# Sums of two weight blocks on VectorE: each tied behind the corrections that precede it in the program

## The chip, the cores and the metric

One core of one Trainium2 chip. The kernel is a single launch; its time is device microseconds of that core, lower is better. A TensorE clock is granted by the throttle and shown by the profile as a share of full speed.

## The reference

A decoder trunk of two layers on 256 tokens of width 2048, in float32: a layer with gated linear attention, a layer with sliding-window attention and sinks, each followed by an MLP of width 8192. What matters here are the large products, all with weights that are read from HBM once:

```python
def sqrelu_mlp(h, w1, w2):
    u = jax.nn.relu(h @ w1)
    return (u * u) @ w2

for layer in range(DEPTH):
    u = rmsnorm(h, norm_mix[layer])
    h = h + mixer(u, ...)                       # GLA in layer 0, windowed attention in layer 1
    h = h + sqrelu_mlp(rmsnorm(h, norm_mlp[layer]), mlp_w1[layer], mlp_w2[layer])
```

## The kernel before

**Weights in two parts.** TensorE multiplies in a reduced float32 format, so each weight block of 512x512 (a tile of 128x2048 in SBUF) is split: ScalarE casts it to a rounded copy `wh`, VectorE subtracts that from the block and leaves the correction `wl`. `halve` does this in two halves of 128x1024 each: two casts (line 116) and two corrections (line 117). Activations are split in the same way. A product of a block with one tile of 128 tokens is then 12 matmuls of 512 columns: for each of four slices k one with `wh`, one with `wl`, one more with `wh` and the activations' small part. The second matmul of each three is the first that needs the correction.

**Rings.** `wh` has 4 tiles of half a block (two blocks), so a block's casts can start only when TensorE is done with the block two before it, half by half. `wl` and the weight tiles `ws` have 3 buffers each.

**Seven products.** Pairs of block columns use Strassen's scheme in Winograd's form: a 2x2 arrangement of blocks b11, b12, b21, b22 needs seven products instead of eight, with sums of weight blocks as operands. A sum is formed in place by VectorE (128x2048, or two halves of 128x1024), and some sums by a DMA that accumulates into the tile `wx`. Besides the seven-product part there are "plain" blocks, which multiply all 256 tokens (24 matmuls). The scheme is written twice:

- `Seven` for the columns of the gated layer's v and r (heads 2 and 3), of two residual projections, and of the MLP's first matrix (`two_columns`, 14 times). The order of its steps is a string, such as `1 21 3 7 5 31 x 20 e 6 2 30 a 4`: a single digit is a product, two digits a plain block, x and the steps 7 and 2 form sums.
- `seven`, for the MLP's second matrix, 16 times: for each of two layers, four groups g of rows, two pairs n of columns. Its order on TensorE is: product 0, plain (2,1), product 2, plain (3,1), products 4 and 6, plain (2,0), plain (3,0), then product 5, product 1 (with b21) and product 3 (with the last sum). The prediction calls the last three products 5, 2 and 4, as `Seven` does; and it calls the b12 product (`product("C", 6, b12)`) by the name of its block.

**Three kinds of sums.** b12 += b22 (lines 307 and 1193), x += b22 (lines 322 and 1198; in the heads and the residual projections a DMA does it) and x += b21 (lines 331 and 1211). The last needs x's product 5 or 6 to have been split first, and b21 to have been loaded; b21 itself is the operand of product 2, and the sum x that of product 4.

**What sets the order.** The program is written in the order of the work; a scheduler puts it into one queue for each engine. `tc.high_priority(offset=WPRI)`, with WPRI = 60, lets an instruction stand ahead of its place by 60 steps of priority; loads, casts, corrections and sums have it, the additions that empty PSUM (lines 1149 and 1150) mostly have not. Each engine runs its own queue in order.

Of the kernel before, what the change touches and what calls it, by code (L numbers as in the profile page):

```python
# [8 lines left out]
F32 = mybir.dt.float32  # L9
# [26 lines left out]
WPRI = 60  # L36
# [15 lines left out]
def yoco_kernel(ctx: ExitStack, tc: tile.TileContext, x, norms, mlp_w1, mlp_w2, a_w_in, w_glr, w_gate, a_g_o, a_w_o,  # L52
                kv_w_k, kv_w_v, kv_g_k, b_w_q, b_g_q, b_sinks, b_w_o, out):
    nc = tc.nc
# [22 lines left out]
    def tick():  # L77
        now[0] += 1
        for fn in due.pop(now[0], ()):
            fn()  # L80

    def mm(o, l, r, start=True, stop=True, **kw):
        nc.tensor.matmul(o, lhsT=l, rhs=r, start=start, stop=stop, **kw)  # L83
# [20 lines left out]
    nc.gpsimd.memset(mhalf, -0.5)  # L104


    def halve(ws, o=C, n=2):

        whs = [wp.tile([P, 2, C], F32R, name="wh", tag="wh", bufs=WHL) for _ in range(2)]
        wl = wp.tile([P, 4, C], F32R, name="wl", tag="wl", bufs=WS)  # L110
        with tc.high_priority(offset=WPRI):
            for k in range(0, 4, n):
                wh = whs[k // 2]
                js, ks = slice(k % 2, k % 2 + n), slice(k, k + n)
                w = ws[k // 2] if isinstance(ws, list) else ws[:, ks, :o]
                nc.scalar.copy(out=wh[:, js, :o], in_=w)  # L116
                nc.vector.tensor_sub(out=wl[:, ks, :o], in0=w, in1=wh.bitcast(F32)[:, js, :o])  # L117
        return [(whs[k // 2][:, k % 2], wl[:, k]) for k in range(4)]

    def split_w(parts, step=4):  # L120
        ws = wp.tile([P, 4, C], F32, name="ws", tag="ws", bufs=WS)
        with tc.high_priority(offset=WPRI):
            for k in range(0, 4, step):
                ks = slice(k, k + step)
                o = 0
                for ap in parts:
                    n = ap.shape[1]
                    nc.sync.dma_start(out=ws[:, ks, o:o + n],
                                      in_=ap[k * P:(k + step) * P].rearrange("(k p) n -> p k n", p=P))
                    o += n  # L130
        return halve(ws, o, min(step, 2))
# [85 lines left out]
    class Seven:  # L217
# [39 lines left out]
        def product(self, b, o, ws):  # L257
            p, st = self.use(b)
            halves = halve(ws)
            for k in range(4):  # L260
                wh, wl = halves[k]
                mm(p, o[0][:, k], wh, st and k == 0, False, skip_group_check=True)
                mm(p, o[0][:, k], wl, False, False, skip_group_check=True)
                mm(p, o[1][:, k], wh, False, k == 3, skip_group_check=True)
            tick()
            return p

        def plain(self, i, j, b0, b1):
            halves = halve(self.load(i, j))
            ps_ = [self.use(b) for b in (b0, b1)]  # L270
            for k in range(4):
                wh, wl = halves[k]
                for t in range(NT):
                    p, st = ps_[t]
                    a, l = self.token(i, t)
                    mm(p, a[:, k], wh, st and k == 0, False, skip_group_check=True)
                    mm(p, a[:, k], wl, False, False, skip_group_check=True)
                    mm(p, l[:, k], wh, False, k == 3, skip_group_check=True)
                if k % 2:
                    tick()  # L280
# [22 lines left out]

        def p7(self, after):
            b12 = self.load(0, 1)
            with tc.high_priority(offset=WPRI):
                nc.vector.tensor_add(out=b12, in0=b12, in1=self.y)  # L307
            after["p7"](self.product("C", self.op(3), b12))

        def ef(self, after):  # L310
# [6 lines left out]
            after["p5"](p)  # L317

        def px(self, after):
            with tc.high_priority(offset=WPRI):  # L320
                for n in range(2):
                    nc.vector.tensor_add(out=self.wx[n], in0=self.wx[n], in1=self.y[:, 2 * n:2 * n + 2])

        def p6(self, after):
            after["p56"](self.product("D", self.op(1), self.wx))

        def p2(self, after):
            b21 = self.load(1, 0)
            with tc.high_priority(offset=WPRI):
                for n in range(2):  # L330
                    nc.vector.tensor_add(out=self.wx[n], in0=self.wx[n], in1=b21[:, 2 * n:2 * n + 2])
            self.product("A", self.token(1, 0), b21)
            if not self.late:
                after["a"](self.banks["A"])

# [616 lines left out]
    def mlp(w1, w2, act, r, gains):  # L952
# [32 lines left out]
        def two_columns(col, es, hs, put, order):  # L985
# [45 lines left out]
            def p4(p):  # L1031
# [5 lines left out]
                      [x[:, 2 * i:2 * i + 2] for i in range(2)],  # L1037
                      lambda: mp.tile([P, 4, C], F32, name="wy", tag="wy", bufs=1))
            z.run({"p1": p1, "p7": p7, "ef": lambda e, f: ef.extend((e, f)), "p5": p5, "p56": p56, "a": p2, "c": p4},
                  order)  # L1040

# [52 lines left out]
        def seven(w, n, op, us, g, acts, gains, sq, nr):  # L1094
# [9 lines left out]
            def load(pool, tag, bufs, i, j):  # L1104
                ws = pool.tile([P, 4, C], F32, name=tag, tag=tag, bufs=bufs)
                with tc.high_priority(offset=WPRI):
                    nc.sync.dma_start(out=ws, in_=block(i, j).rearrange("(k p) n -> p k n", p=P))
                return ws
# [7 lines left out]
            def use(b):  # L1116
                if b in banks:
                    return banks[b], False
                banks[b] = bank([P, C], "ms" if b in "EF" else "acc")
                return banks[b], True  # L1120

            def product(b, o, ws):
                p, st = use(b)
                halves = halve(ws)
                for k in range(4):
                    wh, wl = halves[k]
                    mm(p, op[o][:, 0, k], wh, st and k == 0, False, skip_group_check=True)
                    mm(p, op[o][:, 0, k], wl, False, False, skip_group_check=True)
                    mm(p, op[o][:, 1, k], wh, False, k == 3, skip_group_check=True)
                tick()  # L1130
                return p
# [46 lines left out]
            x = load(mp, "wx", 2, 0, 0)  # L1178
# [7 lines left out]
            y = load(mp, "wy", 1, 1, 1)  # L1186
# [2 lines left out]
            add(x12, banks["E"])  # L1189
            add(x22, banks["F"])  # L1190
            b12 = load(wp, "ws", WS, 0, 1)
            with tc.high_priority(offset=WPRI):
                nc.vector.tensor_add(out=b12, in0=b12, in1=y)
            p = product("D", 4, x)
            add(x21, p)
            sub(x22, product("C", 6, b12))
            with tc.high_priority(offset=WPRI):
                nc.vector.tensor_add(out=x, in0=x, in1=y)
            for i in (2, 3):
                plain(i, 0, "A", "C", i == 2)  # L1200
            p = product("D", 5, x)
# [5 lines left out]
                done(c1)  # L1207
                sub(x21, v)
            b21 = load(wp, "ws", WS, 1, 0)
            with tc.high_priority(offset=WPRI):  # L1210
                nc.vector.tensor_add(out=x, in0=x, in1=b21)  # L1211
            product("A", 1, b21)
            add(x11, banks["A"])
            if g == n + 2 == 3 and not gains:

# [2 lines left out]
                for b in range(2):  # L1218
                    bs = slice(b * T, (b + 1) * T)
                    for k in range(4):  # L1220
                        wh, wl = (w[:, bs] for w in halves[k])
# [14 lines left out]
        for g in range(4):  # L1236
            w = w2[g * D:(g + 1) * D]
# [49 lines left out]
            for n in range(2):  # L1287
                seven(w, n, op, us, g, acts, gains, sq, nr)
# [241 lines left out]
```

## Time and profile before

| | |
|---|---|
| time, median of 3 runs | 2017.83 us (2017.53 to 2018.16) |
| the profiled execution | 2018.76 us, span 2016.8 us |
| TensorE (PE) busy | 2001.5 us, 99% |
| VectorE (DVE) busy | 1752.5 us, 87% |
| ScalarE (ACT) busy | 1308.1 us, 65% |
| GpSimd (POOL) busy | 182.9 us, 9% |
| casts of weight blocks to `wh`, line 116, 128x1024 | 1052 ns each |
| corrections `wl`, line 117, 128x1024 | 1220 to 1240 ns each |
| sums of 128x2048, lines 1198 and 1211 | 2291 ns each, 16 of each kind |
| sums of 128x2048, line 307 (MLP) and 1193 | 2285 ns each, 14 and 16 |
| half sums of 128x1024, lines 322 and 331 | 1218 and 1222 ns each, 28 and 36 |

PE is TensorE's matmuls, PEld its weight loads, which overlap. A row of the timeline has the start in us from the span's start, the duration in us, the engine, the line of the program, the operation and its tiles; x2 at its end marks two like instructions in a row. In brackets stands how long the engine was idle before it, and what ended that. Successive matmuls and successive VectorE operations overlap a little: the start of the next is what counts for rates.

### The profile page before, as it was taken

What the parts mean: (1) busy time and instruction counts of PE and PEld (TensorE: products, weight loads), DVE (VectorE), ACT (ScalarE), POOL (GpSimd) and SP (SyncE); (2) the same over time, 40 slices, a digit from 0 to 9 for tenths busy, and PEclk for the clock granted to TensorE, in tenths of its full rate; (3) what the DMA queues carried; (4) which work ended last, traced back from release to release, by engine and by line L of the source; (5) the groups of instructions that cost most, each with busy time, mean ns of one, the idle gap of its engine ahead of it and who ended that gap; (6) DMA issues with size and microseconds to landing.
All of it is one profiled execution on the core that took longest, in us unless ns stands there. A gap on an engine that the chain in (4) does not pass through costs nothing.

```text
span 2016.8 us, 25788 instructions
## 1 busy us (share of the span) xinstructions
PE 2001.5 (99%) x9714; PEld 1660.9 (82%) x9714; DVE 1752.5 (87%) x1922; ACT 1308.1 (65%) x1724; POOL 182.9 (9%) x199
## 2 busy tenths in 40 slices
PE   9999999999999999999999999999999999999999
PEld 9998888888888888888887878788888888887887
DVE  6698787789989989989999676898889989998998
ACT  6746666667557657656766676666657656755765
POOL 2251110000000000000001121000000000000000
PEclk9999999999999999999999999999999999999999
DMA  8445775796787687778765543687687778778764
GB/s 288 147 157 177 216 222 188 202 291 203 227 273 223 223 264 222 242 241 255 209 202 169 167 135 121 208 285 211 222 261 227 234 245 254 206 230 262 222 225 126
DMA packets 220972, 437.74 MB, mean 217 GB/s; under 512 B 8000, under 2 KB 18512, under 8 KB 218800
## 3 DMA queue, kind: packets, MB, share of 16 engines
q1 hardware_dynamic: 195296, 380.92, 55.4%
q0 software_dynamic: 22464, 53.30, 14.0%
q10 hardware_dynamic: 3088, 1.88, 0.3%
q8 instruction: 76, 1.25, 0.2%
q14 instruction: 48, 0.39, 0.1%
HBM read 429.78 MB, written 6.29 MB: 216 GB/s over the span
## 4 chain that ended last, share of the span: by engine, by line
PE 86%; DVE 7%; ACT 3%; issue 2%; DMA 2%; POOL 0%; SPq 0%; ACTq 0%; POOLq 0%; DVEq 0%
PE acc L83 63%; PE ms L83 14%; PE tp L83 6%; DVE wl L117 3%; PE tp L999 1%; DMA wx<-in_mlp_w_dram 1%; ACT sc L1413 1%; ACT wh L116 1%; DMA ws<-in_a_w_in_dram 1%; DVE wx L1211 0%; PE tp L844 0%; DVE ws L307 0%; DVE sc L1423 0%; PE tp L1345 0%; DVE st L1407 0%
## 5 line engine op out<-in xcount | busy, mean ns | idle before, releaser
L83 PE MATMUL acc<-wh,act 128*128 128x512 f32 x2928 | 938.7, 393 | 0.6 <-DVE xs L1150 0.5
L116 ACT CAST wh<-ws 128x1024 fp32r<-128x1024 f32 x576 | 603.2, 1052 | 339.2 <-PE acc L83 208.2
L117 DVE TENSOR_TENSOR wl<-ws,wh 128x1024 fp32r<-128x1024 f32 x576 | 707.4, 1240 | 100.7 <-ACT wh L116 96.7
L83 PEld LDWEIGHTS acc<-wh,act 128*128 128x128 f32 x2928 | 547.7, 188 | 117.9 <-DVE xs L1150 3.3
L83 PE MATMUL acc<-wl,act 128*128 128x512 f32 x1464 | 570.7, 390 | 1.1 <-DVE wl L117 1.1
L116 ACT CAST wh<-wx 128x1024 fp32r<-128x1024 f32 x272 | 286.0, 1053 | 197.9 <-PE acc L83 140.2
L117 DVE TENSOR_TENSOR wl<-wx,wh 128x1024 fp32r<-128x1024 f32 x272 | 328.0, 1220 | 72.7 <-ACT wh L116 68.5
L83 PEld LDWEIGHTS acc<-wl,act 128*128 128x128 f32 x1464 | 275.1, 188 | 57.0 <-DVE wl L117 1.5
L83 PE MATMUL ms<-wh,act 128*128 128x512 f32 x512 | 166.3, 393 | 0.0
L83 PE MATMUL acc<-act,wh 128*128 128x256 f32 (+1 forms) x640 | 141.4, 308 | 0.5 <-ACT wh L414 0.5
L83 PE MATMUL acc<-wh,ops 128*128 128x512 f32 (+1 forms) x392 | 123.3, 386 | 0.1
L83 PE MATMUL acc<-wh,op 128*128 128x512 f32 x384 | 123.4, 389 | 0.0
L83 PEld LDWEIGHTS ms<-wh,act 128*128 128x128 f32 x512 | 96.1, 188 | 19.5
L83 PEld LDWEIGHTS acc<-act,wh 128*128 128x128 f32 x640 | 104.5, 191 | 6.0 <-ACT wh L414 0.8
L83 PE MATMUL acc<-act,wl 128*128 128x256 f32 x384 | 107.4, 283 | 0.2 <-DVE wl L415 0.2
L83 PE MATMUL ms<-wl,act 128*128 128x512 f32 x256 | 99.7, 390 | 0.0
L83 PE MATMUL tp<-wh,cmb 128*128 128x512 f32 x288 | 94.6, 389 | 0.0
L83 PE MATMUL acc<-wh,cmb 128*128 128x512 f32 x264 | 85.9, 392 | 0.0
L83 PEld LDWEIGHTS acc<-wh,ops 128*128 128x128 f32 x392 | 73.1, 188 | 15.1 <-ACT wh L116 0.6
L83 PEld LDWEIGHTS acc<-wh,op 128*128 128x128 f32 x384 | 72.1, 188 | 15.0
L1112 POOL DMA_DIRECT2D wx<-in_mlp_w_dram x16 | 20.6, 1288 | 656.5 <-DVE wl L117 616.0
L83 PE MATMUL acc<-wl,ops 128*128 128x512 f32 (+1 forms) x196 | 76.3, 389 | 3.1 <-DVE wl L117 3.1
(302 smaller groups left out, 2577.6 us busy)
## 6 DMA issues: line engine op xcount, KB each, us to landing
ws<-in_mlp_w_dram SPq DMA_DIRECT2D x196, 1024.0 KB, 5.4
ws<-in_a_w_in_dram SPq DMA_DIRECT2D x42, 1024.0 KB, 5.1
wy<-in_mlp_w_dram SPq DMA_DIRECT2D x30, 1024.0 KB, 6.6
wx<-in_mlp_w_dram SPq DMA_DIRECT2D x16, 1024.0 KB, 5.2
wx<-in_mlp_w_dram POOLq DMA_DIRECT2D x16, 1024.0 KB, 9.7
ws<-in_b_w_q_dram SPq DMA_DIRECT2D x16, 1024.0 KB, 5.1
ws<-in_a_w_o_dram SPq DMA_DIRECT2D x15, 1024.0 KB, 5.1
ws<-in_b_w_o_dram SPq DMA_DIRECT2D x15, 1024.0 KB, 5.0
```

Of the source, the lines that this page charges most:

```text
L83: nc.tensor.matmul(o, lhsT=l, rhs=r, start=start, stop=stop, **kw)
L116: nc.scalar.copy(out=wh[:, js, :o], in_=w)
L117: nc.vector.tensor_sub(out=wl[:, ks, :o], in0=w, in1=wh.bitcast(F32)[:, js, :o])
L999: nc.tensor.transpose(out=tp[:, k, :], in_=h[:, k * P:(k + 1) * P], identity=ident)
L1112: nc.gpsimd.dma_start(out=ws, in_=block(i, j).rearrange("(k p) n -> p k n", p=P), accum_op=ALU.add)
L1413: nc.scalar.activation(out=sc[:, h], in_=sc[:, h], func=AF.Exp, bias=nmx[:, h:h + 1], scale=f[:, h:h + 1], accum_out=su[:, h:h + 1])
```

## The change

A list `split` now holds the last correction that the program has recorded. A sum is no longer a plain high-priority addition: `add_w` issues it with the same priority, but not before that last correction. Where the program calls the sum of b21 (step 2 of `Seven`, and its counterpart in `seven`), the call of product 2 and the sum have changed places, so that the last recorded correction is that of b21's second half.

```diff
+    split = []
+
+    def add_w(o, a):
+
+        with tc.high_priority(offset=WPRI), tc.issue_after(split[-1].ins):
+            nc.vector.tensor_add(out=o, in0=o, in1=a)
+
     def halve(ws, o=C, n=2):
...
                 nc.scalar.copy(out=wh[:, js, :o], in_=w)
-                nc.vector.tensor_sub(out=wl[:, ks, :o], in0=w, in1=wh.bitcast(F32)[:, js, :o])
+                split[:] = [nc.vector.tensor_sub(out=wl[:, ks, :o], in0=w, in1=wh.bitcast(F32)[:, js, :o])]
...
         def p7(self, after):
             b12 = self.load(0, 1)
-            with tc.high_priority(offset=WPRI):
-                nc.vector.tensor_add(out=b12, in0=b12, in1=self.y)
+            add_w(b12, self.y)
...
         def px(self, after):
-            with tc.high_priority(offset=WPRI):
-                for n in range(2):
-                    nc.vector.tensor_add(out=self.wx[n], in0=self.wx[n], in1=self.y[:, 2 * n:2 * n + 2])
+            for n in range(2):
+                add_w(self.wx[n], self.y[:, 2 * n:2 * n + 2])
...
         def p2(self, after):
             b21 = self.load(1, 0)
-            with tc.high_priority(offset=WPRI):
-                for n in range(2):
-                    nc.vector.tensor_add(out=self.wx[n], in0=self.wx[n], in1=b21[:, 2 * n:2 * n + 2])
             self.product("A", self.token(1, 0), b21)
+            for n in range(2):
+                add_w(self.wx[n], b21[:, 2 * n:2 * n + 2])
...
# in seven():
             b12 = load(wp, "ws", WS, 0, 1)
-            with tc.high_priority(offset=WPRI):
-                nc.vector.tensor_add(out=b12, in0=b12, in1=y)
+            add_w(b12, y)
             p = product("D", 4, x)
             add(x21, p)
             sub(x22, product("C", 6, b12))
-            with tc.high_priority(offset=WPRI):
-                nc.vector.tensor_add(out=x, in0=x, in1=y)
+            add_w(x, y)
...
             b21 = load(wp, "ws", WS, 1, 0)
-            with tc.high_priority(offset=WPRI):
-                nc.vector.tensor_add(out=x, in0=x, in1=b21)
             product("A", 1, b21)
+            add_w(x, b21)
             add(x11, banks["A"])
```

The numbers of instructions stay as they were; what moves is their order, on VectorE above all. In the rows below a number behind a tile's name tells one tile of that name from another.

VectorE's queue in a `seven` with n = 0 (layer 0, g = 2), before, from the corrections of product 5 (`wl_7308`) on; `wl_7331` is product 2's, `wl_7351` product 4's, `wl_7374` that of the first product of the next `seven`, and `xs_2953<-acc_7073` is the addition of x11, which needs product 2 to have ended on TensorE:

```order
L117 TENSOR_TENSOR wl_7308<-wx_7071,wh_7306 128x1024
L117 TENSOR_TENSOR wl_7308<-wx_7071,wh_7307 128x1024
L1211 TENSOR_TENSOR wx_7071<-wx_7071,ws_7326 128x2048
L117 TENSOR_TENSOR wl_7331<-ws_7326,wh_7329 128x1024
L117 TENSOR_TENSOR wl_7331<-ws_7326,wh_7330 128x1024
L117 TENSOR_TENSOR wl_7351<-wx_7071,wh_7349 128x1024
L1149 TENSOR_TENSOR v0_3719<-acc_7197,v0_3719 128x512
L117 TENSOR_TENSOR wl_7351<-wx_7071,wh_7350 128x1024
L117 TENSOR_TENSOR wl_7374<-wx_7369,wh_7372 128x1024
L117 TENSOR_TENSOR wl_7374<-wx_7369,wh_7373 128x1024
L1149 TENSOR_TENSOR xs_2953<-acc_7073,xs_2953 128x512
```

The same place after; lines have moved by some numbers, L124 is the correction, L112 the sum, L1153 the addition from PSUM, and product 2's correction is now `wl_7330`:

```order
L124 TENSOR_TENSOR wl_7308<-wx_7071,wh_7306 128x1024
L124 TENSOR_TENSOR wl_7308<-wx_7071,wh_7307 128x1024
L124 TENSOR_TENSOR wl_7330<-ws_7326,wh_7328 128x1024
L124 TENSOR_TENSOR wl_7330<-ws_7326,wh_7329 128x1024
L112 TENSOR_TENSOR wx_7071<-wx_7071,ws_7326 128x2048
L1153 TENSOR_TENSOR v0_3719<-acc_7197,v0_3719 128x512
L1153 TENSOR_TENSOR xs_2953<-acc_7073,xs_2953 128x512
L124 TENSOR_TENSOR wl_7351<-wx_7071,wh_7349 128x1024
L124 TENSOR_TENSOR wl_7351<-wx_7071,wh_7350 128x1024
L124 TENSOR_TENSOR wl_7374<-wx_7369,wh_7372 128x1024
```

The sum for product 4 has moved behind both corrections of product 2, and the additions of v and x11 now stand between it and product 4's first correction. In the `seven`s with g = 3 an addition of v to x12 stands there in place of that of x11.

VectorE's queue earlier in the same `seven`, before: `wl_7200` belongs to `product("D", 4, x)`, `wl_7221` that of b12, `wl_7244` plain (2,0); the two additions from `ms` need plain (3,1) to have ended:

```order
L117 TENSOR_TENSOR wl_7200<-wx_7071,wh_7199 128x1024
L1198 TENSOR_TENSOR wx_7071<-wx_7071,wy_7138 128x2048
L117 TENSOR_TENSOR wl_7221<-ws_7194,wh_7219 128x1024
L1149 TENSOR_TENSOR xs_3029<-ms_7112,xs_3029 128x512
L117 TENSOR_TENSOR wl_7221<-ws_7194,wh_7220 128x1024
L117 TENSOR_TENSOR wl_7244<-ws_7240,wh_7242 128x1024
```

The same place after:

```order
L124 TENSOR_TENSOR wl_7200<-wx_7071,wh_7199 128x1024
L124 TENSOR_TENSOR wl_7221<-ws_7194,wh_7219 128x1024
L1153 TENSOR_TENSOR xs_3029<-ms_7112,xs_3029 128x512
L1153 TENSOR_TENSOR xs_3029<-ms_7113,xs_3029 128x512
L124 TENSOR_TENSOR wl_7221<-ws_7194,wh_7220 128x1024
L112 TENSOR_TENSOR wx_7071<-wx_7071,wy_7138 128x2048
L124 TENSOR_TENSOR wl_7244<-ws_7240,wh_7242 128x1024
```

The sum x += b22 has moved from ahead of b12's corrections to behind them, directly ahead of plain (2,0)'s first.

VectorE's queue in a `seven` with n = 1 (layer 0, g = 2), before, where the b12 sum of the next `two_columns` (L307) stands between the two corrections of product 2 (`wl_7621`):

```order
L1211 TENSOR_TENSOR wx_7369<-wx_7369,ws_7616 128x2048
L117 TENSOR_TENSOR wl_7621<-ws_7616,wh_7619 128x1024
L307 TENSOR_TENSOR ws_7754<-ws_7754,wy_7733 128x2048
L1149 TENSOR_TENSOR v1_3720<-acc_7487,v1_3720 128x512
L117 TENSOR_TENSOR wl_7621<-ws_7616,wh_7620 128x1024
```

After, that b12 sum stands behind the corrections of b22 (`wl_7737`, step 3 of the `two_columns`):

```order
L124 TENSOR_TENSOR wl_7737<-wy_7733,wh_7735 128x1024
L124 TENSOR_TENSOR wl_7737<-wy_7733,wh_7736 128x1024
L112 TENSOR_TENSOR ws_7754<-ws_7754,wy_7733 128x2048
L1153 TENSOR_TENSOR xs_3267<-acc_7508,xs_3267 128x512
L124 TENSOR_TENSOR wl_7760<-ws_7754,wh_7758 128x1024
```

So nothing stands between product 2's two corrections any more. On SyncE's queue of loads two neighbours change places at each hand-over from one pair of columns to the next: b21's load and that of the next b22 (`wy`). GpSimd's order is unchanged.

## The prediction

> **What bounds the kernel now.** I read the page first: busy times and the chain of work that ended last, with the granted clock.
>
> ```profile
> PE 2001.5 (99%) x9714; PEld 1660.9 (82%) x9714; DVE 1752.5 (87%) x1922; ACT 1308.1 (65%) x1724; POOL 182.9 (9%) x199
> PEclk9999999999999999999999999999999999999999
> PE 86%; DVE 7%; ACT 3%; issue 2%; DMA 2%; POOL 0%; SPq 0%; ACTq 0%; POOLq 0%; DVEq 0%
> ```
>
> TensorE is the bound, so the change can win only the time in which TensorE waits for corrections, and can lose whatever new wait it makes there. Second, the waits, and the rows of TensorE where one ends:
>
> ```profile
> PE acc L83 <- DVE wl L117: 4.1, 8, 0.6
> PE tp L83 <- DVE wl L117: 0.9, 2, 0.5
> 574.40 0.50 PE L83 MATMUL acc<-wl,ops 128*128 128x512 f32 x1 [0.51 <-DVE wl L117]
> ...
> 1836.55 0.50 PE L83 MATMUL acc<-wl,ops 128*128 128x512 f32 x1 [0.51 <-DVE wl L117]
> ```
>
> All matmul waits for corrections together are 5.0 us in 10 pieces. Six of them are alike (first and last shown), one for each `seven` with n = 1 and g below 3. The timeline of one of the six explains it:
>
> ```profile
> 905.38 1.22 DVE L117 TENSOR_TENSOR wl<-ws,wh 128x1024 fp32r<-128x1024 f32 x1
> 906.51 2.29 DVE L307 TENSOR_TENSOR ws<-ws,wy 128x2048 f32<-128x2048 f32 x1
> 908.71 0.68 DVE L1149 TENSOR_TENSOR v<-acc,v 128x512 f32<-128x512 f32 x1
> 909.31 1.22 DVE L117 TENSOR_TENSOR wl<-ws,wh 128x1024 fp32r<-128x1024 f32 x1
> 910.58 0.50 PE L83 MATMUL acc<-wl,ops 128*128 128x512 f32 x1 [0.51 <-DVE wl L117]
> ```
>
> Product 2's second correction waits behind the next b12 sum; TensorE resumes 0.05 after its end (909.31 + 1.22 = 910.53). The matmul three ahead of it started at 909.23 and the pitch is 0.227, so it was due at 909.91: 0.67 lost. The starts also give VectorE's pitches: correction 1.13, sum 2.20, addition 0.60.
>
> **The clock of a block's second correction.** Third, one `seven` with n = 0 around products 5, 2 and 4, by engine:
>
> ```profile
> 864.30 0.39 PE L83 MATMUL acc<-wh,act 128*128 128x512 f32 x1
> 864.53 0.39 PE L83 MATMUL acc<-wh,op 128*128 128x512 f32 x1
> 869.74 0.62 PE L83 MATMUL acc<-wh,ops 128*128 128x512 f32 x2
> 870.19 0.39 PE L83 MATMUL acc<-wl,ops 128*128 128x512 f32 x1
> 864.73 1.06 ACT L116 CAST wh<-ws 128x1024 fp32r<-128x1024 f32 x1 [1.66 <-PE acc L83]
> 862.77 2.29 DVE L1211 TENSOR_TENSOR wx<-wx,ws 128x2048 f32<-128x2048 f32 x1
> 864.98 2.35 DVE L117 TENSOR_TENSOR wl<-ws,wh 128x1024 fp32r<-128x1024 f32 x2
> 867.25 1.22 DVE L117 TENSOR_TENSOR wl<-wx,wh 128x1024 fp32r<-128x1024 f32 x1
> ```
>
> TensorE starts product 5 at 864.53. Only then is plain (3,0) off the ring, and product 2's second cast runs (864.73, 0.43 after plain (3,0)'s last matmul began). It ends at 865.79; the correction can start some 0.04 later, 865.83, and VectorE is free for a next operation at 866.96. So whatever is tied behind a block's second correction starts no earlier than 2.43 after the block ahead of it began on TensorE. A sum of 2.20 ends its turn at 4.63, and a correction behind that is usable at 4.63 + 1.22 + 0.05 = 5.90. If the blocks ahead are two products (24 matmuls, 5.44), the next block's first `wl` matmul is due at 5.67: too late. If one of them is a plain block (8.16 + 0.23 = 8.39), 2.49 is left. Before, the sum used the hole ahead of this correction (862.77 to 864.98), where VectorE has nothing else to do.
>
> **The change part by part.**
>
> *Product 4's sum in `seven`, 16 times.* Sum from 866.96; its turn ends at 869.16, the addition of v's at 869.76. Then the addition of x11 stands ahead of product 4's first correction, and it needs product 2's last matmul, begun at 869.74: released at 870.17 by the same 0.43, turn over at 870.77. Correction until 871.99, TensorE resumes at 872.04 against 870.19: 1.85 lost. With g = 3 an addition that waits for nothing stands there, and the cast decides: sum ends 869.25, cast 869.29 to 870.35, correction 870.39 to 871.61, TensorE 871.66: 1.47. Sum 12 x 1.85 + 4 x 1.47 = 28.1. The second half's correction follows 1.13 later, the six matmuls of a half take 1.36, so it adds nothing.
>
> *x += b22 in `seven`, 16 times*, now behind b12's second correction; ahead of plain (2,0) stand two products.
>
> ```profile
> 848.35 1.06 ACT L116 CAST wh<-ws 128x1024 fp32r<-128x1024 f32 x1 [1.66 <-PE ms L83]
> 853.82 0.39 PE L83 MATMUL acc<-wl,act 128*128 128x512 f32 x1
> ```
>
> Cast until 849.41, correction 849.45, sum 850.58, plain's correction 852.78 to 854.00, usable at 854.05 against 853.82: 0.23 each, 3.7 in all. The two additions now ahead of that second correction fit in before 849.45 (plain (3,1) has ended by 848.35 and they take 1.20, so 849.55 at worst: 0.10 more each, an end for the range).
>
> *Product 4's half sums in `two_columns`, 14 times*, tied behind product 2, with product 6 ahead and plain (3,0) next.
>
> ```profile
> 941.95 1.05 ACT L116 CAST wh<-ws 128x1024 fp32r<-128x1024 f32 x1 [1.66 <-PE acc L83]
> 939.92 1.22 DVE L331 TENSOR_TENSOR wx<-wx,ws 128x1024 f32<-128x1024 f32 x1
> 941.06 1.22 DVE L117 TENSOR_TENSOR wl<-ws,wh 128x1024 fp32r<-128x1024 f32 x1
> 947.42 0.39 PE L83 MATMUL acc<-wl,act 128*128 128x512 f32 x1
> ```
>
> A half sum has a pitch of 1.14. Cast until 943.00, correction 943.04, sums from 944.17 to 946.45, plain's correction until 947.67, usable 947.72 against 947.42: 0.30 each, 4.2 in all.
>
> *The same in the four `Seven`s of heads and residuals*, where product 4 itself follows product 2 and one addition (vp) stands between:
>
> ```profile
> 258.99 1.23 DVE L117 TENSOR_TENSOR wl<-ws,wh 128x1024 fp32r<-128x1024 f32 x1 [1.50 <-ACT wh L116]
> 261.53 0.68 DVE L764 TENSOR_TENSOR vp<-tp,vp 128x512 f32<-128x512 f32 x1
> 263.37 0.39 PE L83 MATMUL acc<-wl,act 128*128 128x512 f32 x1
> ```
>
> 258.99 + 1.13 + 2 x 1.14 + 0.60 = 263.00, usable 264.27 against 263.37: 0.90 each, 3.6.
>
> *Removed:* the b12 sum between product 2's corrections, 6 x 0.67 = 4.0 gained.
>
> *The other ties* (b12 sums, and step x's sums) stand behind blocks with a plain block among the two, by the clock above 2.49 early, or 1.29 with two additions in between. Taken at nothing; without that cover each would cost its turn of up to 2.20.
>
> *Transfers.* b21's load and `wy`'s change places. No row shows that order; the nearest are
>
> ```profile
> 888.43 0.37 SPq L238 DMA_DIRECT2D wy<-in_mlp_w_dram  x1
> 891.90 0.37 SPq L1107 DMA_DIRECT2D ws<-in_mlp_w_dram  x1
> wy<-in_mlp_w_dram SPq DMA_DIRECT2D x30, 1024.0 KB, 6.6
> ```
>
> A `wy` issued with b21 at 891.90 lands at 898.5, and its first reader before was the sum at 906.51: 8 us of cover. Nothing; if it were late, both ends are 0 and the 3.47 between the two issues.
>
> Sum: 28.1 + 3.7 + 4.2 + 3.6 - 4.0 = 35.6 us. The profiled execution took 2018.76 (span 2016.8 and 1.96 around it); it would take 2054.4. The median of the three runs lies 0.93 lower, so the forecast is 2053.
>
> **A stall and the clock.** New stalls of 1.85 might cost more than themselves if TensorE's clock fell after them. The trace has one stall of that size, and the clock behind it:
>
> ```profile
> 1267.17 0.63 PE L1432 MATMUL tp<-ident,sc 128*128 128x128 f32 x4 [1.61 <-DVE pv L1440]
> 1267.10:1272.00 4.90, 4.83 (x22) 2.91 (x23) 2.88 (x3) 1.66 (x3) 0.00 (x0) 1.00 0.95 319
> ```
>
> After 1.61 us idle the granted clock is 1.00. The Trainium skill ("TensorE: Matmul & The Clock Gate", What's actually happening) says that TensorE falls to half its clock after at least one idle window of about 3.4 us, and that the window runs freely. By that rule the sum stays as it is, since no stall here reaches 3.4; were the clock halved anyway, the fourth rival would follow.
>
> **The rivals.**
> 1. *Faster.* Only the six stalls go: 2053 - 39.6 = 2013. It holds if product 4's first correction starts by 870.19 - 1.27 = 868.92, so the sum by 868.92 - 0.60 - 2.20 = 866.12, and with x11's addition behind it. For it: VectorE idles 2.83 us before product 5's corrections in this place, so total work is no obstacle. Against it: the cast's 866.96 is set by TensorE, and the queue puts x11's addition ahead.
> 2. *Only product 4 pays.* The 34 smaller stalls, 0.23 to 0.90 long, are hidden by some slack that I do not see: 2053 - 11.5 = 2042. For it: 0.23 is near the error of adding such rows.
> 3. *More.* At the 30 places of x += b22 and of the half sums one more addition (0.60) ends up in the path: 2053 + 18 = 2071. For it: additions from PSUM wait in the same queue; against: the queue shows none there.
> 4. *The clock drops* for the product behind each of the 16 stalls, 2.72 more each: 2053 + 43.5 = 2097. Against it: the clock row above.
> 5. *No effect*, if the tie moved nothing on the path: 2018. The queues show that it does move.
>
> ```profile
> 860.14 2.60 DVE L117 TENSOR_TENSOR wl<-wx,wh 128x1024 fp32r<-128x1024 f32 x2 [2.83 <-ACT wh L116]
> ```
>
> (That row is the 2.83 of the first rival.)
>
> **How the numbers follow.** Forecast 0.70, since each term is a chain of three to five rows against a due time; rival 2 0.10, rival 3 0.08, rival 4 0.02, faster 0.07, no effect 0.03. A measurement of this kernel can tell about 0.2% (4 us) from no change. Slower by more than that is 0.70 + 0.10 + 0.08 + 0.02 = 0.90, faster 0.07, the same 0.03. The range takes in rivals 2 and 3 with some 7 us below the first and 3 above the second, for the 0.10 and 0.60 of unsure turns: 2035 to 2074; outside lie rivals 1, 4 and 5 (0.12).
>
> **What would show it.** In the profile after: TensorE waits on corrections rise from 5 us to some 40; 16 matmuls of product 4 with a stall near 1.85 (1.47 with g = 3), 16 of plain (2,0) near 0.23, 14 of plain (3,0) near 0.30, four of product 4 in `Seven` near 0.90; none at product 2's second half; VectorE's busy time unchanged. I am wrong if the sum of line 1211's counterpart starts well before 2.43 after product 5's first matmul, or if product 4's correction does not follow x11's addition.

## The result

The changed kernel takes 2062.24 us (median of 4 runs, 2061.47 to 2063.27) against 2017.99 us: 44.3 us or 2.2% slower, ratio 1.0218, 95% interval 1.0205 to 1.0231. The forecast was 2053 us, 35 us slower, with a range of 2035 to 2074: the direction and the mechanism came out as forecast, and the loss is 9 us larger. The profiled execution took 2063.27 us, its span is 2061.3.

The page of the kernel after, the lines that answer to those shown of before (busy times, granted clock, chain of work):

```profile
PE 2019.1 (98%) x9714; PEld 1659.3 (80%) x9714; DVE 1752.9 (85%) x1922; ACT 1300.8 (63%) x1724; POOL 183.5 (9%) x199
PEclk9999999999999999999999999999999999999999
PE 79%; DVE 13%; ACT 3%; issue 3%; DMA 1%; POOL 0%; ACTq 0%; DVEq 0%; POOLq 0%
```

VectorE does the same work (1752.9 against 1752.5 us) over a longer span, and has 13% of the chain where it had 7%. That is the mark of work that got later, not longer. TensorE's own waits, kernel after (total us, times, longest):

```profile
PE acc L83 <- DVE wl L124: 22.2, 29, 1.1
PE acc L83 <- ACT wh L123: 6.1, 18, 0.4
PE tp L83 <- DVE wl L124: 2.5, 3, 1.0
PE acc L83 <- ACT wh L418: 1.5, 1, 1.5
```

Waits for corrections rose from 5.0 to 24.7 us, and waits for casts of weight blocks (line 123), not in the list before, came to 6.1. These figures are smaller than the loss, because a row's bracket counts the idle time only from the end of the matmul ahead, 0.39 after its start, while the next one was due 0.227 after that start. The full price of a stall is read from starts: the distance of two successive matmuls less the pitch, which is 0.227 for 128x512 (for the narrower matmuls, the median distance of their form before). Counted so, distances that exceed the pitch by 0.06 or more come to 46.9 us before and 89.7 after: 42.8 of the 44.5 us between the spans.

The place of product 4, kernel after, n = 0 and g = 2, VectorE, ScalarE and TensorE:

```profile
880.37 1.23 DVE L124 TENSOR_TENSOR wl<-ws,wh 128x1024 fp32r<-128x1024 f32 x1
882.18 1.23 DVE L124 TENSOR_TENSOR wl<-ws,wh 128x1024 fp32r<-128x1024 f32 x1 [0.59 <-ACT wh L123]
883.33 2.28 DVE L112 TENSOR_TENSOR wx<-wx,ws 128x2048 f32<-128x2048 f32 x1
885.53 0.69 DVE L1153 TENSOR_TENSOR v<-acc,v 128x512 f32<-128x512 f32 x1
886.54 0.69 DVE L1153 TENSOR_TENSOR xs<-acc,xs 128x512 f32<-128x512 f32 x1 [0.33 <-PE acc L83]
887.14 2.35 DVE L124 TENSOR_TENSOR wl<-wx,wh 128x1024 fp32r<-128x1024 f32 x2
881.10 1.06 ACT L123 CAST wh<-ws 128x1024 fp32r<-128x1024 f32 x1 [0.76 <-PE acc L83]
885.72 1.05 ACT L123 CAST wh<-wx 128x1024 fp32r<-128x1024 f32 x1 [3.57 <-DVE wx L112]
886.11 0.39 PE L83 MATMUL acc<-wh,ops 128*128 128x512 f32 x1
886.83 0.50 PE L83 MATMUL acc<-wh,ops 128*128 128x512 f32 x1 [0.33 <-ACT wh L123]
888.41 0.50 PE L83 MATMUL acc<-wl,ops 128*128 128x512 f32 x1 [1.09 <-DVE wl L124]
888.75 0.63 PE L83 MATMUL acc<-wh,ops 128*128 128x512 f32 x2
```

Follow it down. Product 2's second cast waits for TensorE (881.10), its correction for the cast (882.18). The sum starts at 883.33, and that is the forecast's 2.43 after product 5's first matmul (880.90). Product 4's first cast waits for the sum (885.72, idle 3.57). TensorE is ready for product 4 at 886.34 (886.11 and the pitch) and gets the cast at 886.83: 0.49 lost. The addition of x11 waits for product 2's end (886.54), only then the correction comes, and TensorE resumes at 888.41 where 887.06 would follow: 1.35 more (1.36 at most of the other places). Together 1.84, against the 1.85 forecast. The matmul after that comes 0.34 later instead of 0.227: another 0.11, not forecast.

### The profile page after: what moved, and what is told of

It reads as the page before. It is cut to its first block, busy times and chain, and to the rows that moved or that the text cites. A ratio compares the mean times of both kernels' runs of the same rounds, so it can differ in the third digit from the quotient of the medians.

```text
span 2061.3 us, 25817 instructions
## 1 busy us (share of the span) xinstructions
PE 2019.1 (98%) x9714; PEld 1659.3 (80%) x9714; DVE 1752.9 (85%) x1922; ACT 1300.8 (63%) x1724; POOL 183.5 (9%) x199
## 4 chain that ended last, share of the span: by engine, by line
PE 79%; DVE 13%; ACT 3%; issue 3%; DMA 1%; POOL 0%; ACTq 0%; DVEq 0%; POOLq 0%
PE acc L83 60%; PE ms L83 11%; DVE wl L124 6%; PE tp L83 5%; DVE wx L112 2%; ACT wh L123 1%; PE tp L1003 1%; DVE ws L112 1%; ACT sc L1414 1%; DVE xs L1153 1%; DMA wx<-in_mlp_w_dram 1%; PE tp L848 0%; DVE sc L1424 0%; PE tp L1346 0%; DMA xt<-in_x_dram 0%
## 5 line engine op out<-in xcount | busy, mean ns | idle before, releaser
L124 DVE TENSOR_TENSOR wl<-ws,wh 128x1024 fp32r<-128x1024 f32 x576 | 704.3, 1241 | 131.2 <-ACT wh L123 125.2
L123 ACT CAST wh<-wx 128x1024 fp32r<-128x1024 f32 x272 | 281.3, 1052 | 296.2 <-PE acc L83 166.3
L124 DVE TENSOR_TENSOR wl<-wx,wh 128x1024 fp32r<-128x1024 f32 x272 | 324.9, 1220 | 80.1 <-ACT wh L123 77.4
L83 PE MATMUL acc<-wh,ops 128*128 128x512 f32 (+1 forms) x392 | 127.5, 390 | 5.3 <-ACT wh L123 5.3
```

What stands on the lines that cost most here:

```text
L124: split[:] = [nc.vector.tensor_sub(out=wl[:, ks, :o], in0=w, in1=wh.bitcast(F32)[:, js, :o])]
```

## Experiments

Eleven kernels, in four groups; each group was timed beside the kernel before, and a loss is counted from those runs. A tie means that a sum is issued with `add_w`, behind the last correction recorded. Two ties of the change were never made alone: the one of the b12 sum in `seven`, and the one of the half sums x += b22 in `Seven`.

### Each tie alone

`only_x21` is the kernel before with one tie:

```diff
-            with tc.high_priority(offset=WPRI):
-                nc.vector.tensor_add(out=x, in0=x, in1=b21)
             product("A", 1, b21)
+            add_w(x, b21)
```

> The kernel before, with one tie alone: in seven, the sum x += b21 stands behind both corrections of product 2 (16 places). Theory A (the late sum itself is what costs; terms add up): the trace of the full change shows at these places 0.48 + 1.36 + 0.11 us of TensorE standing still, with g = 3 a little less, 28.9 us in all; this kernel should be 28 to 30 us slower than before, about 2047, with the six stalls of 0.67 us in product 2 still there. Rival B (the ties work together, the sum is late only because the other ties load VectorE ahead of it): under 20 us. Rival C (nearly all of the 44 us is made here, the small terms are an artefact of reading): over 38 us.

2048.78 us, ratio 1.0150 (1.0133 to 1.0167): 30.3 us slower. Rivals B and C are out, and theory A's two waits stand in the trace, here at the first n = 1.

```profile
578.31 0.51 PE L83 MATMUL acc<-wh,ops 128*128 128x512 f32 x1 [0.32 <-ACT wh L123]
579.90 0.51 PE L83 MATMUL acc<-wl,ops 128*128 128x512 f32 x1 [1.09 <-DVE wl L124]
```

That the total is theory A's as well is in part luck. It expected the six stalls of product 2 to stay, and they are gone from this trace (the matmul at 576.92 follows at the pitch), 4.7 us gained: the b12 sum, though not tied, has taken the slot that x += b21 left, ahead of both corrections (570.06). In the profiled execution late operands cost about as much: 4.3 us behind a cast that waited 5.12 for a load of wx (before 1836.60), and some 2.5 at two of the 16 places where the cast came later still (921.59 and 1516.87).

`only_xy` ties x += b22 in seven alone (`add_w(x, y)`).

> The kernel before, with one tie alone: in seven, x += b22 stands behind b12's second correction (16 places); b12's own sum stays early. Prediction's term: 3.7 us. Theory A: the cast of b12's second half still bounds the chain, plus 0.11 us of slow restart at each stall, so 16 x 0.35 = 5 to 6 us. Rival B (the tie costs 0.73 with n = 0 and 0.40 with n = 1 by itself, as in the trace of the full change): 9.0 us. If 5 to 6 comes out, the rest of the 9.0 comes from the tied b12 sum, which fills the stretch of VectorE ahead of it.

2022.88 us, ratio 1.0022 (1.0013 to 1.0032): 4.4 us slower. This is nearer the 5 to 6 of theory A than 9.0. At 15 of the 16 places its trace has the forecast's chain, with a stall of 0.24 against the 0.23 forecast, and 0.11 behind it:

```profile
513.95 1.23 DVE L124 TENSOR_TENSOR wl<-ws,wh 128x1024 fp32r<-128x1024 f32 x1 [0.30 <-ACT wh L123]
515.09 2.28 DVE L112 TENSOR_TENSOR wx<-wx,wy 128x2048 f32<-128x2048 f32 x1
517.30 2.35 DVE L124 TENSOR_TENSOR wl<-ws,wh 128x1024 fp32r<-128x1024 f32 x2
518.57 0.50 PE L83 MATMUL acc<-wl,act 128*128 128x512 f32 x1
518.91 0.39 PE L83 MATMUL acc<-wh,act 128*128 128x512 f32 x1
```

The places bear theory A out; the total is again helped by luck. The six stalls of product 2 are gone here too (4.7 gained), against 1.3 lost at the sixteenth place (1067.79), 2.8 in small pieces at product 4, and some at the start of the kernel.

VectorE still waits 0.30 for b12's cast ahead of the correction at 513.95, so the cast bounds it. In the full change, at a place with n = 0, it does not:

```profile
858.70 2.28 DVE L112 TENSOR_TENSOR ws<-ws,wy 128x2048 f32<-128x2048 f32 x1
860.89 2.35 DVE L124 TENSOR_TENSOR wl<-wx,wh 128x1024 fp32r<-128x1024 f32 x2
863.16 1.22 DVE L124 TENSOR_TENSOR wl<-ws,wh 128x1024 fp32r<-128x1024 f32 x1
864.30 1.28 DVE L1153 TENSOR_TENSOR xs<-ms,xs 128x512 f32<-128x512 f32 x2
865.50 1.22 DVE L124 TENSOR_TENSOR wl<-ws,wh 128x1024 fp32r<-128x1024 f32 x1
866.63 2.29 DVE L112 TENSOR_TENSOR wx<-wx,wy 128x2048 f32<-128x2048 f32 x1
868.83 2.36 DVE L124 TENSOR_TENSOR wl<-ws,wh 128x1024 fp32r<-128x1024 f32 x2
870.11 0.50 PE L83 MATMUL acc<-wl,act 128*128 128x512 f32 x1 [0.46 <-DVE wl L124]
```

There is no idle time in this row of VectorE operations, where only_xy idles 1.10 (before 511.23) and 0.30. The tied b12 sum stands at its head (858.70) and has used that time, so all that follows is late by the queue itself: the cast was done at 864.07 + 1.06 = 865.13, the correction starts at 865.50. The stall is 0.62 and 0.11; with n = 1, where the cast bounds, 0.29 and 0.11.

`only_half` ties the half sums of Seven's step 2 alone.

> The kernel before, with one tie alone: in Seven, step 2's half sums x += b21 behind product 2's corrections (14 places of two_columns ahead of plain (3,0), 4 places ahead of product 4). Prediction's terms: 4.2 + 3.6 = 7.8 us. Theory A, from the trace of the full change: 14 x 0.22 (0.08 to 0.14 and the 0.11 behind it) + 3 x 1.01 + 0.3 = 6.4 us. Rival B (the half sums cost nothing, the small stalls are made good later): under 2 us.

2029.57 us, ratio 1.0057 (1.0042 to 1.0072): 11.1 us slower, more than either figure. In its trace distances of 0.06 and more over the pitch come to 55.1 us, 8.2 more than before; the other 2.3 of the 10.5 between the spans lie in smaller differences. Beyond the places named in the expectation, four of the six old stalls of 0.67 at product 2 have become 0.87 there, and one wait of 0.69 for a late load of wx in `two_columns` is new.

`only_b12` ties Seven's b12 sum alone, the part that was to take the six stalls away.

> The kernel before, with one tie alone: in Seven, step 7's sum of b12 behind the corrections of b22 (18 places). Prediction: a gain of 4.0 us, nothing lost. Theory A: the six stalls of 0.67 + 0.11 go (4.7 us gained), but at the start of each MLP (first two_columns) the tied sum pushes low additions ahead of product 5's correction, 1.7 to 2.0 us lost twice, so 0 to 2 us faster than before. Rival B: 4 to 5 us faster, since the loss at the MLP's start needs another tie.

2025.45 us, ratio 1.0037 (1.0024 to 1.0051): 7.0 us slower, and neither figure held. The six stalls at product 2 are gone. But the starts of the two MLPs lost 1.9 each, and six new stalls came up, one for each g above 0:

```profile
664.85 2.29 DVE L1199 TENSOR_TENSOR ws<-ws,wy 128x2048 f32<-128x2048 f32 x1
667.05 2.35 DVE L124 TENSOR_TENSOR wl<-ws,wh 128x1024 fp32r<-128x1024 f32 x2
669.33 1.28 DVE L1290 TENSOR_TENSOR act<-tp,act 128x512 fp32r<-128x512 f32 x2
670.15 0.30 PE L1005 MATMUL tp<-ident,h 128*128 128x128 f32 x1 [0.86 <-DVE act L1290]
```

The transposes of h wait for a bank of PSUM, which is free only after a subtraction (L1290). The queue holds that behind the *untied* b12 sum of `seven` (L1199), which now stands behind both of the corrections of `wl<-wx` and not between them. For three of the six the profile names a cast that ends at the same time as the subtraction; in `b12s` below, where that sum is tied too, all six are gone. So a tie of one sum shifted the scheduler's choice for others.

### The same sums, one half block earlier; x11; all but one

`all_first` is the full change with `tc.issue_after(split[-2].ins)` for `split[-1].ins` (and `split` kept as a list): each sum behind the first of the two corrections.

> The full change with one difference: each sum is tied behind the first of the two corrections ahead of it, not the second. All sums, loads and products are the same. Theory A (a block's second cast waits until TensorE has ended the block two before it, so what stands behind the second correction starts 2.43 us after the block ahead; behind the first correction it starts 1.3 to 1.6 us earlier): the stalls of product 4, of plain (2,0) and of plain (3,0) go, the gain of 4.7 at product 2 stays, the 3.8 us lost at the two MLP starts stay, some late wx loads stay; about 2017 to 2021, 40 us faster than the change. Rival B (any move of the sums behind corrections costs it, because VectorE has no room there): above 2040.

2023.9 us, ratio 1.0029 (1.0017 to 1.0040): 5.4 us slower than before, 38 us faster than the change, and 3 us above the 2017 to 2021 of theory A. The same place, VectorE and TensorE:

```profile
866.65 1.23 DVE L124 TENSOR_TENSOR wl<-ws,wh 128x1024 fp32r<-128x1024 f32 x1
867.80 2.28 DVE L112 TENSOR_TENSOR wx<-wx,ws 128x2048 f32<-128x2048 f32 x1
870.00 1.22 DVE L124 TENSOR_TENSOR wl<-ws,wh 128x1024 fp32r<-128x1024 f32 x1
871.13 0.69 DVE L1153 TENSOR_TENSOR v<-acc,v 128x512 f32<-128x512 f32 x1
871.74 3.49 DVE L124 TENSOR_TENSOR wl<-wx,wh 128x1024 fp32r<-128x1024 f32 x3
873.01 0.51 PE L83 MATMUL acc<-wl,ops 128*128 128x512 f32 x1
```

Sums and corrections are the same in number and length; only the sum's turn has passed from behind the cast that waits for TensorE into the time in which VectorE would wait for it. Product 4 now loses 0.13 and 0.11 at 14 of its 16 places, some 4 us that theory A left out. Rival B is out.

`x21_first` is only_x21 with the tie at the first correction.

> The kernel before with one tie alone, in seven: x += b21 behind the first correction of product 2 instead of ahead of both (behind the second it cost 30 us). Theory A: product 4's first correction then ends about 0.8 us before it is due, no stall: same as before within 2 us. Rival B (the sum is late by any place behind product 2's corrections): 10 us or more slower.

2026.13 us, ratio 1.0040 (1.0028 to 1.0053): 7.6 us slower, against 30.3 with the tie at the second, but not the nothing that was expected. With n = 0 the stalls are gone. With n = 1 and g below 3 they are there in full:

```profile
568.56 2.28 DVE L314 TENSOR_TENSOR ws<-ws,wy 128x2048 f32<-128x2048 f32 x1
570.76 1.22 DVE L124 TENSOR_TENSOR wl<-ws,wh 128x1024 fp32r<-128x1024 f32 x1
572.17 1.22 DVE L124 TENSOR_TENSOR wl<-ws,wh 128x1024 fp32r<-128x1024 f32 x1 [0.20 <-ACT wh L123]
573.32 2.28 DVE L112 TENSOR_TENSOR wx<-wx,ws 128x2048 f32<-128x2048 f32 x1
...
578.40 0.50 PE L83 MATMUL acc<-wl,ops 128*128 128x512 f32 x1 [1.09 <-DVE wl L124]
```

The next b12 sum (L314) has taken the slot, and the scheduler put x += b21 behind the second correction although the tie asked only for the first: `issue_after` says not before, it does not say right behind. Where the sum did stand behind the second correction, the stall came back; that is the mechanism again. The six stalls at product 2 are gone (4.7 gained), since L314 stands ahead of both corrections; with 12 us lost at the six places that gives the 7.6 within 0.3.

`all_x11l` is the full change with `add(x11, ...)` issued behind product 4's corrections.

> The full change, but the addition of x11 stands behind product 4's corrections. By the trace of the change product 4's first correction could start at the end of its cast, 0.33 us earlier, at the 12 places with g below 3: 12 x 0.33 = 4 us faster than the change, about 2058. Prediction's step: 12 x (1.85 - 1.47) = 4.6 us. Rival B (x11's wait for product 2 is what makes product 4 late): 20 us or more faster than the change. Rival C (nothing: the cast alone decides): the same as the change within 1 us.

2059.02 us, ratio 1.0202 (1.0188 to 1.0216): 40.5 us over its own runs of before, 3.8 less than the change, near the 4 of the trace, though the two intervals overlap. Product 4's second piece fell from 1.36 to 1.03. x11's addition is a small part; the late sum is the large one.

`all_but_x21` is the full change with x += b21 of `seven` left as before.

> The full change without the tie of x += b21 in seven (that sum stands as before, all others tied). If the terms add up: 2062 - 29 to 30 = 2032 to 2033, 14 to 15 us slower than before. The ties made alone so far came to 30.3 + 4.4 + 11.1 + 7.0 = 52.8, more than the 44 of all together, so some of these are not additive; if the interplay lies in x += b21, this kernel comes out above 2040, else near 2032.

2037.73 us, ratio 1.0097 (1.0082 to 1.0113): 19.2 us slower, so x += b21 accounts for 25 of the 44 when it is taken away last, and for 30 when it is made first. The trace's count at its 16 places, 29, lies between. The parts are not additive, and the interplay is not in this tie alone: the result lies between the two cases of the expectation. The ties made alone come to more than the 44 although three of them have the gain at product 2, which can be had only once, because each alone also has losses that the full change lacks (the six stalls of only_b12, the late operands of only_x21). Some of what is left over here is the start: TensorE's first wait for a cast from the first loads (`ACT wh L418` above) was 0.5 us before, 1.5 in the change and 1.9 in the profile of this kernel, while nothing there was edited.

### Towards a version that gains

`best` is all_first with x += b21 of `seven` in two halves, one behind each correction of product 2, and the b12 sum of each MLP's first `two_columns` untied.

> all_first with two edits: in seven the sum x += b21 is made in two halves, the first behind product 2's first correction and the second behind its second, and the first two_columns of each MLP keeps its b12 sum untied. Theory A: all_first still stands 0.13 + 0.11 us at product 2's second half at 16 places (3.8 us; the whole sum of 2.20 is ahead of that correction, half of it would be in time) and 1.9 us at each MLP start (3.8 us); without these, 2024 - 7.6 = 2016 to 2017, 1 to 3 us faster than the kernel before. Rival B (these stalls are made good later): 2022 to 2025. Rival C (half sums push later work back): slower than all_first.

2020.38 us, ratio 1.0010 (1.0001 to 1.0019): 2.2 us slower than its runs of before, where all_first was 5.4 slower. That is 3.2 us better, short of the 7 expected, and the two intervals just overlap. The expectation put the 0.13 of all_first at product 2's second half, and that reading was wrong: by the rows above it is product 4's first correction. Two halves don't help there; it became 0.23 and 0.11, as product 2's second cast still comes first and a half sum, v's addition and the correction follow it.

`b12s` ties the b12 sums alone, in `Seven` (not at the MLPs' starts) and in `seven`.

> The kernel before with the b12 sums alone tied, behind the second correction ahead of them: in Seven (but not in the first two_columns of an MLP) and in seven. With Seven's tie alone the kernel was 7.0 us slower; its trace shows the 4.7 us gained at product 2, 3.9 lost at the MLP starts and six new stalls of 0.9 to 1.0 where TensorE's transposes of h wait for a subtraction that stands behind seven's b12 sum. Theory A: with seven's b12 sum tied too these six go, with the starts untied the 3.9 go: 3 to 5 us faster than before, 2014 to 2016. Rival B (the six stalls come from Seven's tie itself): 2018 to 2020. Rival C (something else than these stalls makes the 7.0): 2021 or more.

2018.09 us, ratio 0.9998 (0.9989 to 1.0006): the same as before, the figure of rival B, though not for its reason: the six new stalls of only_b12 and the starts' losses are gone from the trace, so they did come from the untied sum of `seven` and from the starts. But of the 4.7 that should then be gained the profiled span shows 1.9 (2014.9), and the runs nothing; the profiled execution (2016.92) was 1.2 us below their median. The trace shows where some of it went. Product 4's first correction is now 0.03 late at most places, and with the 0.11 behind each of these small waits (534.13 to 534.47) that makes 2.5 us; 1.3 is lost at one plain (2,0) (1064.40). Why those corrections came later isn't settled.

`mix` is best with x += b21 of `seven` put back ahead of product 2.

> best with x += b21 of seven put back to its old place, ahead of product 2's corrections; all other sums tied behind the first correction ahead of them, the first two_columns of each MLP untied. In the profile of best a stall of 0.23 + 0.11 us is left at product 4 at most of the 16 places, since VectorE's turns for the two half sums, product 2's second correction and v's addition still lie between product 2's second cast and product 4's first correction. Theory A: without it 4 to 5 us less than best, 2015 to 2016.5, 1.5 to 3 us faster than before. Rival B: as b12s, whose trace was also 4 us short of stalls at product 2 and which was measured the same as before: 2018 within 1 us.

2018.3 us, ratio 0.9998 (0.9989 to 1.0007): as rival B had it. No version was found that beats the kernel before.

## Why the prediction was right, and where it was short

The terms, in us, forecast and as counted from the starts of matmuls in the trace after (each with the 0.11 of slow restart):

| term | forecast | trace after |
|---|---|---|
| product 4 in `seven`, 16 places | 28.1 | 29.0 |
| plain (2,0), x += b22, 16 places | 3.7 | 9.1 |
| plain (3,0) in `two_columns`, 14 places | 4.2 | 2.8 |
| product 4 in heads and residuals, 4 places | 3.6 | 3.3 |
| starts of the two MLPs | 0 | 3.9 |
| product 2's six stalls removed | -4.0 | -4.7 |
| sum | 35.6 | 43.4 |

The terms err in both directions, so the 9 us between forecast and result are a balance: 5.4 at plain (2,0) and 3.9 at the MLPs' starts were missing, 1.4 at plain (3,0) was too much. The spans differ by 44.5; 1.0 of what is missing is the first wait for loaded weights (0.5 before, 1.5 after), at the start of the kernel.

- *The clock of a second correction* held. all_first shows it as the cause: moved to the other side of that correction, the same sums cost 38 us less.
- *Product 4* came out as worked: 1.85, made of 0.49 for the cast and 1.36 for the correction, and 0.11 of restart; 12 x 1.96 = 23.5 in all, and 5.5 for the four places with g = 3. The forecast's share for x11's addition, 12 x 0.38 = 4.6, is near the 12 x 0.33 of the trace and the 3.8 of all_x11l, whose interval doesn't settle it alone.
- *Plain (2,0)* is the term that was mis-sized. "The two additions now ahead of that second correction fit in before 849.45" took VectorE's queue as before, with a free stretch there. The change's own b12 sum had moved into that stretch (858.70 above). With n = 0 the stall became 0.62 and not 0.23; where the stretch is free, as in only_xy, 0.24 was measured.
- *"The other ties ... taken at nothing"* failed at the MLPs' starts. The clock gave 1.29 us of cover with two additions in between; there were four 128x512 subtractions (line 1080, parts of the products' operands) directly ahead of product 5's corrections (1.07 lost, and 0.10 behind it). Another 0.58 is a wait for a cast (470.91): ScalarE waited 1.64 for the tied sum (464.97) and then ran without a pause up to that cast.

```profile
467.80 1.22 DVE L124 TENSOR_TENSOR wl<-ws,wh 128x1024 fp32r<-128x1024 f32 x1
468.93 0.68 DVE L1080 TENSOR_TENSOR op<-e,op 128x512 fp32r<-128x512 f32 x1
469.53 0.69 DVE L1080 TENSOR_TENSOR ops<-e,ops 128x512 fp32r<-128x512 f32 x1
470.13 1.29 DVE L1080 TENSOR_TENSOR ops<-u,ops 128x512 fp32r<-128x512 f32 x2
471.34 2.35 DVE L124 TENSOR_TENSOR wl<-wx,wh 128x1024 fp32r<-128x1024 f32 x2
472.61 0.50 PE L83 MATMUL tp<-wl,cmb 128*128 128x512 f32 x1 [0.96 <-DVE wl L124]
```

- *Removed*: the six stalls went as forecast, but not for this tie alone. They are also gone in only_x21, only_xy and x21_first, where the b12 sums are not tied.
- *Transfers*: the exchange of b21's and `wy`'s loads shows nowhere in the waits. One load did come late in the change, a cast in `two_columns` that waited 2.76 us for wx (947.89) and cost 0.77 and 0.11; before, two such places cost 0.58 and 0.64.
- *The rivals*: faster, only product 4, no effect are all out by the table. The third, one more addition at each of 30 places (18 us), is out by its size: those places came to 11.9 against 7.9 forecast, and what moved into the queue ahead of plain (2,0) was the b12 sum. The fourth, the falling clock, is out for this kernel by the clock row of the page, by the granted clock of 1.0 in all four runs, and by a stretch with a stall of product 4 in it (kernel after, busy times of PE, PEld, DVE, ACT, POOL, then granted clock, DMA share, GB/s):

```profile
540.00:546.00 6.00, 4.59 (x20) 3.25 (x19) 5.68 (x7) 5.45 (x6) 0.00 (x0) 1.00 0.73 224
```

The rival was nearer than the prediction had it, though. In only_x21 the clock did fall once, behind product 4's two stalls at 1516.87 and 1518.12 (idle 1.04 and 0.76 by their rows):

```profile
1515.00:1518.00 3.00, 1.33 (x5) 0.55 (x3) 3.00 (x5) 2.23 (x3) 0.00 (x0) 1.00 0.42 74
1520.00:1522.00 2.00, 2.00 (x6) 1.61 (x5) 2.00 (x3) 1.04 (x1) 1.22 (x1) 0.50 0.87 268
```

For 3.4 us (1518.67 to 1522.08) the granted clock was 0.50 and the matmuls came 0.427 apart, 1.6 us lost. The same pair of stalls in x21_first (1505.83 and 1507.09) left the clock at 1.00; what tells the two cases apart is not shown.

The Trainium skill ("TensorE: Matmul & The Clock Gate", What's actually happening) has the clock fall after at least one idle window of about 3.4 us. The change agrees with it: TensorE's longest waits there are 1.1 to 1.6 us, and the clock is 1.00. If such a window is taken as one unbroken wait, only_x21 does not agree, since its clock fell after waits of 1.04 and 0.76 us; the measurement decides.

## What to carry to other kernels

Work tied behind an operation inherits what that operation waits for: before moving it, ask which engine releases that operation, and count from there to the next due time. A free stretch of an engine that is 87% busy is a resource with a place; two moves that each fit into it alone need not fit together, so the cover of each term is to be read from the order after the whole change. A stall that is easy to see (six of 0.67 here) can be the cheaper side of an order that hides a dozen larger ones. And a total that agrees with a theory is not yet the theory's: in only_x21 and only_xy a gain and a loss that nobody expected cancelled, and only the trace's places, one by one, bear the theory out.

## What the runs showed of the hardware

After 30 of the 32 waits of TensorE for a correction that the change's profile lists, the second matmul followed 0.34 us after the first and not 0.227 (888.41 to 888.75 above; 518.57 to 518.91 in only_xy). Such a stall therefore costs 0.11 us more than the time until TensorE resumes; with some 50 stalls in the change that is 5 us. The two exceptions are near the end of the kernel (2052.05 and 2053.19), where a narrower matmul followed after 0.22. A short wait pays it too: in b12s one of 0.03 was followed by the same 0.34. Why the second matmul is late no run here shows.

TensorE's granted clock fell to 0.50 for 3.4 us after two stalls that lay 1.26 us apart and left TensorE idle for 1.04 and 0.76 us (only_x21, above).
